# A list schedule with a margin on every transfer's landing time, and new tables of due times and earliest starts

## The chip, the cores and the metric

The kernel runs on one core of a Trainium2 chip. The metric is the device time of one execution in microseconds (us); of several executions the median is given. The engines are named as in the profile: PE multiplies matrices and PEld loads its weights, DVE and ACT do elementwise work, POOL and SP issue DMA transfers here and little else.

## The reference

One decoder block over 512 positions and 1024 channels, all in float32. `x` is (1, 512, 1024), `mem` (1, 256, 1024), and the inner width of the feed-forward part is 2816.

```
h = RMSNorm(x);  proj = h @ w_in          # 1024 x 9216: B, C, v | u, ug | q | three gates
y_a = (B * conv3(C * v)) @ w_a_out
y_b = swish(LayerNorm(conv31(u * sigmoid(ug)) + bias)) @ w_b_out
k, v = RMSNorm(mem) @ w_kv;  y_c = attention(q, k, v; 4 heads) @ w_att_out
m = sum_i sigmoid(gate_i + b_gate) * y_i
x = x + m @ w_o
f = RMSNorm(x) @ w_up;  gt, up = split(conv3(f))
out = RMSNorm(x + (silu(gt) * up) @ w_down)
```

All convolutions are depthwise and causal along the positions.

## The kernel before, in words

**Products.** A float32 product is made of three products of a faster format. A weight tile of 128x1024 is cast to its high part on ACT (`wh`, the tile `whi`, line 583), the low part is the difference on DVE (`wl`, the tile `wlo`, line 587), and the activations are split in the same way (`fh` and `fl`, lines 672 and 676; for the conformer branch by halves, lines 1459 and 1463). PE then adds up high times high, high times low and low times high (`multiply`, the matmuls at line 760).

**Quads.** The large projections go by quads: two column blocks by two row blocks of a weight are multiplied with seven products in place of eight, in the manner of Strassen. A quad `q` has the units (q,1), (q,2), (q,5), (q,6), (q,7), (q,4), (q,3), each of 24 matmuls of 256 columns, and the units of two neighbouring quads are interleaved. A unit's weight tile is a block as it stands in memory or the sum of two or more blocks. The four loads of a quad are `u`, `v`, `s` and `r`. Some sums are made by an accumulating DMA that POOL issues (`more`, line 708), which needs the earlier split of the same tile done. The results leave the PSUM banks by the reads `r1` to `r7` (`quad_reads`, lines 788 to 803 among them). The quads' names: `glu` and `cv` and `bb` for the short convolution's and the conformer's inputs, `q`, `gate`, `mq` for `w_b_out`, `up` and `down`; `wo` and `merge` are the plain products with `w_o` and `w_att_out`.

**Buffers.** Weights land in a ring of six slots (`wf`), in places also in the rings `sb` and `lf`; loads are issued by SP (`fetch_job`, line 613), the accumulating transfers by POOL. The split parts `whi` and `wlo` have four buffers each. A load goes out when its slot has been read for the last time, which is mostly the end of a `wl`.

**What sets the order.** PE's order is written out by hand (`seq`). Everything else is a job with an engine, a cost, the jobs that it comes after, and the slots that it takes. `latest_starts` works back from PE's order to a due time for each job and adds a shift from the table `LATER`, by the kind of job ("DVE wl up 3"). `run` then goes forward in a model of the time: of all jobs that are ready it takes the one that could start first, and of equals the one due first. The table `AHEAD` holds a kind of job back until so many us before its due time. For a transfer the model knows a cost and a latency (`LOAD, MORE = 1.42, 2.55` and `LOAD_LATENCY, MORE_LATENCY = 3.1, 3.4`), and lets SP and POOL share the bandwidth:

```
            ends[key] = free[e] + latency
            for k in dict.fromkeys(users.get(key, ())):
                waits[k] -= 1
                ready_at[k] = max(ready_at.get(k, 0.0), ends[key])
```

What comes out of `run` is only an order: the jobs' functions are called in it, and `issue_in_program_order` makes each engine issue its instructions as they were written. On the chip an engine waits only for the data and buffers that its next instruction needs, so a model time that is off shows as an instruction that stands too early in its engine's queue and holds up those behind it.

Of the kernel before, what the change touches and what calls it, by code (L numbers as in the profile page):

```python
# [67 lines left out]
TABLE_LOAD, TABLE_WAIT = 1.28, 3.0  # L68
SEEN = {"PE": 0.2, "ACT": 0.14, "DVE": 0.12}
# [11 lines left out]
    "ACT kh": 35, "ACT mgh a": -12.9, "ACT mgh c": -228, "ACT mgh d": -361.4, "ACT mgh e": -100,  # L81
    "ACT mgh g": 251.8, "ACT mh": -59.6, "ACT msq": 103.3, "ACT oh": -327, "ACT pth": 35,
# [6 lines left out]
    "ACT rt": -218.2, "ACT sg": -115, "ACT sigmoid": 1235, "ACT silu": -4.5, "ACT sq": -69,  # L89
    "ACT sr": -334, "ACT swish": 252, "ACT tap 1": -214.4, "ACT tap 2": -191, "ACT tap 3": -547.5,  # L90
# [8 lines left out]
    "ACT wn wo 0": -774.4, "ACT x root": 121, "ACT xroot": -5.5, "ACT xsq": -18, "ACT xsquare": 15,  # L99
# [8 lines left out]
    "DVE low": 39.7, "DVE m scale": -418, "DVE mgl a": 159, "DVE mgl b": 325.5, "DVE mgl d": 11,  # L108
    "DVE mgl e": 647.4, "DVE mgl g": -351, "DVE ml": 15, "DVE ms c": -142, "DVE ms d": -3.5,
    "DVE ms e": 328, "DVE msum": -143, "DVE mu fold": -89, "DVE mu low": -614, "DVE mu sum": -395,  # L110
    "DVE ol": -34, "DVE pn": -193, "DVE ptl": -147, "DVE ql": -1183.6, "DVE r2 bb": -176.3,
# [5 lines left out]
    "DVE rd f": -4, "DVE rd g": 51.4, "DVE sc": -297.1, "DVE sum": -988.2, "DVE tap 1": -30,  # L117
    "DVE tap 2": 25.4, "DVE tap 3": 51.2, "DVE top": -7.9, "DVE tot1": -8, "DVE tot2": -44,
    "DVE um": -1259, "DVE var fold": 4.7, "DVE var sum": -23.3, "DVE vl": 737, "DVE weigh": 547,
# [18 lines left out]
    "POOL s7 up": -142, "POOL wadd e": -277, "POOL wadd x": 2.1, "POOL wadd y": -65,  # L138
# [6 lines left out]
}  # L145

AHEAD = {
    "ACT fh h b00": 80, "ACT fh h b11": 150, "ACT fh h t4": 40, "ACT fh h t6": 40,
    "ACT fh h2 t4": 2, "ACT fh h2 t5": 5, "ACT fh h2 t6": 40, "ACT fh y b00": 10, "ACT fh y b10": 2,
    "ACT fh y t6": 80, "ACT m root": 40, "ACT mgh a": 2, "ACT mgh b": 40, "ACT mgh c": 2,  # L150
    "ACT mgh e": 5, "ACT pth": 40, "ACT qh": 20, "ACT r1 bb": 150, "ACT r1 q": 10, "ACT r1 up": 5,
    "ACT r4 gate": 5, "ACT r4 q": 2, "ACT r5 cv": 2, "ACT r5 gate": 40, "ACT r5 glu": 80,
    "ACT r5 q": 150, "ACT r5 up": 20, "ACT r6 bb": 5, "ACT r6 cv": 150, "ACT r6 gate": 20,
    "ACT r6 mq": 150, "ACT r6 q": 40, "ACT r6 up": 20, "ACT rb": 5, "ACT rh": 5, "ACT rm": 150,
# [53 lines left out]
class Jobs:  # L208
# [2201 lines left out]
```

## Time and profile before

Three runs took 941.35, 933.9 and 929.17 us; the median is 933.9. The profile belongs to another execution, the fastest that is known:

| | |
|---|---|
| median of three runs | 933.9 us |
| the profiled execution's own time | 926.63 us |
| its span | 924.8 us |
| mean granted clock of PE | 0.998 |
| PE busy | 911.2 us (99%), 6821 instructions |
| DVE busy | 849.1 us (92%), 973 instructions |
| ACT busy | 681.4 us (74%), 933 instructions |
| POOL busy | 137.2 us (15%), 165 instructions |
| DMA | 196.91 MB, 213 GB/s over the span |

The 1.8 us between 926.63 and 924.8 lie around the span. PE is busy nearly throughout, so what a change of the order can move is the idle time of PE, and that is read from the rows that give, for a PE instruction, how long it waited and for whom.

### The profile page before, as it was taken

How to read it: one execution, taken by the hardware profiler on the slowest of the kernel's cores; microseconds unless marked ns; L12 is line 12 of the kernel's file. 1: busy time of each engine (PE TensorE's matmuls, PEld its weight loads, DVE VectorE, ACT ScalarE, POOL GpSimd, SP SyncE). 2: the span in 40 equal slices, each digit the busy share in tenths (PEclk: the TensorE clock that was granted, in tenths of full speed). 3: DMA queues.
4: the chain of work that ended last, by engine and by line, in shares of the span. 5: the costliest groups of instructions: out<-in, count | busy, mean ns of one | idle time of the engine just before them, and what ended most of it. 6: DMA issues, size and time to landing. Idle time of an engine off the chain costs nothing.

```text
span 924.8 us, 17087 instructions
## 1 busy us (share of the span) xinstructions
PE 911.2 (99%) x6821; PEld 860.7 (93%) x6821; DVE 849.1 (92%) x973; ACT 681.4 (74%) x933; POOL 137.2 (15%) x165
## 2 busy tenths in 40 slices
PE   9999999999999999999999999999999999999996
PEld 8999999999989999999899997898999999988885
DVE  7898999999989999999876999987998889999977
ACT  7577988887988888569647983766766766765555
POOL 0011121100010121111100211121121111002400
PEclk9999999999999999999999999999999999999999
DMA  9999789764579798998957999899999786689962
GB/s 361 372 261 195 168 179 196 179 152 91 144 178 249 145 194 197 220 222 209 216 128 204 213 286 313 217 236 294 272 253 235 166 170 147 179 287 322 253 123 91
DMA packets 55951, 196.91 MB, mean 213 GB/s; under 512 B 6336, under 2 KB 6464, under 8 KB 55872
## 3 DMA queue, kind: packets, MB, share of 16 engines
q0 software_dynamic: 22608, 81.54, 49.6%
q1 hardware_dynamic: 32544, 113.23, 33.8%
q8 instruction: 53, 0.87, 0.4%
q10 hardware_dynamic: 720, 1.06, 0.3%
q14 instruction: 26, 0.21, 0.1%
HBM read 191.60 MB, written 4.19 MB: 212 GB/s over the span
## 4 chain that ended last, share of the span: by engine, by line
PE 84%; DVE 6%; DMA 5%; issue 2%; ACT 1%; SPq 0%; ACTq 0%; DVEq 0%; POOLq 0%
PE bank L760 52%; PE bank L535 6%; PE bank L536 6%; PE bank L534 6%; PE bank L1558 3%; PE bank L1559 3%; PE bank L1560 3%; DMA wf<-in_w_in 3%; DVE wlo L587 2%; PE bank L1017 2%; DMA wf<-in_w_up 2%; DVE upc L1514 1%; PE bank L1792 1%; DVE gtc L1514 1%; ACT whi L583 1%
## 5 line engine op out<-in xcount | busy, mean ns | idle before, releaser
L583 ACT CAST whi<-wf 128x1024 fp32r<-128x1024 f32 x204 | 212.0, 1043 | 101.3 <-PE bank L760 36.9
L587 DVE TENSOR_TENSOR wlo<-wf,whi 128x1024 fp32r<-128x1024 f32 x198 | 238.3, 1211 | 26.9 <-ACT whi L583 26.6
L1326 ACT ACTIVATE tp<-u,pk 128x510 f32<-128x510 f32 (+22 forms) x184 | 118.8, 705 | 2.8 <-DVE acc L1333 2.4
L1333 DVE TENSOR_TENSOR acc<-acc,tp 128x1022 f32<-128x1022 f32 (+22 forms) x92 | 109.1, 1188 | 4.1 <-ACT tp L1326 2.4
L708 POOL DMA_DIRECT2D wf<-in_w_in x50 | 44.4, 895 | 242.7 <-DVE wlo L587 163.0
L760 PE MATMUL bank<-ft6h,whi 128*128 128x256 f32 (+1 forms) x250 | 68.8, 276 | 1.1 <-ACT gt L788 1.1
L760 PE MATMUL bank<-ft4h,whi 128*128 128x256 f32 (+1 forms) x249 | 68.7, 276 | 0.9 <-DVE uu L540 0.9
L760 PE MATMUL bank<-ft5l,whi 128*128 128x256 f32 x248 | 68.7, 277 | 0.6 <-DVE ft5l L676 0.6
L760 PE MATMUL bank<-ft7h,whi 128*128 128x256 f32 x248 | 68.6, 277 | 0.7 <-ACT g L803 0.7
L760 PE MATMUL bank<-ft6h,wlo 128*128 128x256 f32 x248 | 68.7, 277 | 0.2 <-DVE wlo L587 0.2
L760 PE MATMUL bank<-fb10h,whi 128*128 128x256 f32 x248 | 68.7, 277 | 0.0
L760 PE MATMUL bank<-ft6l,whi 128*128 128x256 f32 x248 | 68.7, 277 | 0.0
L760 PE MATMUL bank<-fb00h,whi 128*128 128x256 f32 (+1 forms) x250 | 68.7, 276 | 0.0
L760 PE MATMUL bank<-fb11h,whi 128*128 128x256 f32 x248 | 68.7, 277 | 0.0
L760 PE MATMUL bank<-fb00l,whi 128*128 128x256 f32 x248 | 68.6, 277 | 0.0
L760 PE MATMUL bank<-ft5h,whi 128*128 128x256 f32 (+1 forms) x251 | 68.6, 275 | 0.0
L760 PE MATMUL bank<-ft4l,whi 128*128 128x256 f32 x248 | 68.6, 277 | 0.0
L760 PE MATMUL bank<-ft7l,whi 128*128 128x256 f32 x248 | 68.5, 276 | 0.0
L760 PE MATMUL bank<-ft7h,wlo 128*128 128x256 f32 x248 | 68.5, 276 | 0.0
L760 PE MATMUL bank<-ft4h,wlo 128*128 128x256 f32 x248 | 68.5, 276 | 0.0
L760 PE MATMUL bank<-fb11l,whi 128*128 128x256 f32 x248 | 68.5, 276 | 0.0
L760 PE MATMUL bank<-fb11h,wlo 128*128 128x256 f32 x248 | 68.5, 276 | 0.0
(400 smaller groups left out, 3157.7 us busy)
## 6 DMA issues: line engine op xcount, KB each, us to landing
wf<-in_w_in SPq DMA_DIRECT2D x53, 512.0 KB, 5.8
wf<-in_w_in POOLq DMA_DIRECT2D x50, 512.0 KB, 6.4
wf<-in_w_up SPq DMA_DIRECT2D x30, 512.0 KB, 7.7
wf<-in_w_up POOLq DMA_DIRECT2D x27, 512.0 KB, 7.3
wf<-in_w_down SPq DMA_DIRECT2D x15, 512.0 KB, 6.1
wf<-in_w_att_out SPq DMA_DIRECT2D x8, 512.0 KB, 4.2
wf<-in_w_a_out SPq DMA_DIRECT2D x8, 512.0 KB, 4.5
wf<-in_w_b_out SPq DMA_DIRECT2D x8, 512.0 KB, 6.0
```

The costliest lines, as they stand in the source:

```text
L534: nc.tensor.matmul(ps, s_hi, w_hi, start=start, stop=False, skip_group_check=again)
L535: nc.tensor.matmul(ps, s_hi, w_lo, start=False, stop=False, skip_group_check=again)
L536: nc.tensor.matmul(ps, s_lo, w_hi, start=False, stop=stop, skip_group_check=again)
L583: nc.scalar.copy(parts[0], src())
L587: nc.vector.tensor_tensor(lo, src(), hi.bitcast(F32), op=ALU.subtract)
L708: nc.gpsimd.dma_start(out=tiles[key], in_=block(w, col[c], k), accum_op=ALU.add)
L760: nc.tensor.matmul(ps[:, c, part], w[:, k, at], a[k][:, part], start=first and n == 0 and part.start == 0, stop=k == 3 and n == 2, skip_gr ...
L1326: nc.scalar.activation(two(("tp", p, s))[:, j, s:], two(("u", p))[:, j, : SEQ - s], AF.Copy, scale=weight(j),)
L1333: nc.vector.tensor_tensor(a, a, two(("tp", p, s))[:, :, s:], op=ALU.add)
L1558: nc.tensor.matmul(ps, w_hi[:, i, at], hi, start=first, stop=False)
L1559: nc.tensor.matmul(ps, w_hi[:, i, at], lo, start=False, stop=False)
L1560: nc.tensor.matmul(ps, w_lo[:, i, at], hi, start=False, stop=last)
```

## The change

A transfer lands later in the model by a margin, in both places where `run` sets its end: 1.2 us for a load of SP and 2.0 us for an accumulating transfer of POOL. The second of these places is where a transfer that is under way is slowed by one of the other queue. Both tables `LATER` and `AHEAD` have other numbers throughout; one line of each is kept here.

```diff
@@ -66,6 +66,7 @@
 TABLE_LOAD, TABLE_WAIT = 1.28, 3.0
+MARGIN = {"SP": 1.2, "POOL": 2.0}
 SEEN = {"PE": 0.2, "ACT": 0.14, "DVE": 0.12}
@@ -74,116 +75,118 @@
 LATER = {
-    "ACT kh": 35, "ACT mgh a": -12.9, "ACT mgh c": -228, "ACT mgh d": -361.4, "ACT mgh e": -100,
...
 AHEAD = {
...
+    "DVE fl h t6": 20, "DVE fl h t7": 10, "DVE fl h2 t5": 80, "DVE fl h2 t6": 5,
...
@@ -385,7 +388,7 @@
                     free[slowed] = self.moved(slowed, start)
-                    ends[other] = free[slowed] + self.jobs[other][4]
+                    ends[other] = free[slowed] + self.jobs[other][4] + MARGIN[slowed]
@@ -396,7 +399,7 @@
-            ends[key] = free[e] + latency
+            ends[key] = free[e] + latency + MARGIN.get(e, 0.0)
```

The program that comes out computes the same. PE's order is word for word the same, with 6693 rows. Of DVE's 899 jobs nearly all stand at another place or beside other neighbours. ACT loads its function tables 10 times and not 11. All lines behind the new one are numbered one or three higher.

**SP, at the loads of `w_b_out` and `w_o`** (the conformer branch's last product and the mixer's, from about half of the span on). The load for the unit (mq 1,1) is `wf_5876` before and `wf_5958` now; the quad's fourth load, r of (mq 1), is `wf_6235` before and `wf_6350` now. Before:

```order
L613 DMA wf_5780<-in_w_b_out 128x1024
L613 DMA wf_5844<-in_w_b_out 128x1024
L613 DMA wf_5876<-in_w_b_out 128x1024
L613 DMA wf_5888<-in_w_b_out 128x1024
L613 DMA wf_5922<-in_w_b_out 128x1024
L613 DMA wf_5958<-in_w_b_out 128x1024
L613 DMA wo_6183<-in_w_o 128x1024
L613 DMA wo_6192<-in_w_o 128x1024
L613 DMA wf_6226<-in_w_b_out 128x1024
L613 DMA wf_6235<-in_w_b_out 128x1024
```

After:

```order
L616 DMA wf_5780<-in_w_b_out 128x1024
L616 DMA wf_5845<-in_w_b_out 128x1024
L616 DMA wf_5881<-in_w_b_out 128x1024
L616 DMA wf_5891<-in_w_b_out 128x1024
L616 DMA wf_5926<-in_w_b_out 128x1024
L616 DMA wf_5958<-in_w_b_out 128x1024
L616 DMA wo_6181<-in_w_o 128x1024
L616 DMA wf_6190<-in_w_o 128x1024
L616 DMA wf_6224<-in_w_b_out 128x1024
L616 DMA wo_6232<-in_w_o 128x1024
L616 DMA wf_6312<-in_w_o 128x1024
L616 DMA wf_6350<-in_w_b_out 128x1024
```

The block that the unit (mq 1,1) multiplies was third and is sixth now, and the last load of `w_b_out` goes out behind four loads of `w_o` where there were two.

**ACT, at the same place** (the swish of the conformer branch, line 1424 before, and the casts behind it: `fb00h` is the activations' high part that (mq 1,1) needs, in two halves, and `whi` the weights'). Before:

```order
L1424 ACT_TABLE_LOAD
L1424 ACTIVATE acc_1093<-acc_1093,pk 128x512 x2
L1424 ACTIVATE acc_2140<-acc_2140,pk 128x512 x2
L1459 CAST ft5h_6030<-y_6002 128x512
L1459 CAST fb00h_6033<-acc_1093 128x512
L583 CAST whi_6038<-wf_5876 128x1024
L1459 CAST ft5h_6030<-y_6002 128x512
L1459 CAST fb00h_6033<-acc_2140 128x512
```

After:

```order
L1427 ACTIVATE acc_1093<-acc_1093,pk 128x512 x2
L1427 ACTIVATE acc_2144<-acc_2144,pk 128x512 x2
L586 CAST whi_6027<-wf_5958 128x1024
L1462 CAST fb00h_6032<-acc_1093 128x512
L1462 CAST fb00h_6032<-acc_2144 128x512
L1462 CAST ft5h_6039<-y_6035 128x512
L586 CAST whi_6066<-wf_5780 128x1024
```

The cast of the unit's weights now stands ahead of both halves of `fb00h`. On DVE the difference `wlo_6028` likewise stands ahead of `fb00l`, whose second half comes after `ft5l` and one more `wlo`.

**DVE, between the last quad of bb and the first of gate** (`B` from the bank is the read r7 of (bb,1); the `wlo` behind it belong to the units named in the text above, and `acc` with `tp` are taps of the conformer's convolution of 31 steps). Before:

```order
L540 SCALAR_TENSOR_TENSOR B_4509<-bank_4518,B_4509 128x2x256
L587 TENSOR_TENSOR wlo_4779<-wf_4091,whi_4778 128x1024
L1527 TENSOR_TENSOR C_4335<-C_4335,V_4263 128x1024
L1438 TENSOR_TENSOR yal_4817<-ya_3986,yah_4682 128x1024
L587 TENSOR_TENSOR wlo_4815<-wf_4442,whi_4814 128x1024
L1514 SCALAR_TENSOR_TENSOR ya_4819<-C_4335,pk,ya_4819 128x511
L1514 SCALAR_TENSOR_TENSOR ya_4819<-C_4335,pk,ya_4819 128x510
L587 TENSOR_TENSOR wlo_4849<-wf_4676,whi_4848 128x1024
```

After:

```order
L543 SCALAR_TENSOR_TENSOR B_4505<-bank_4510,B_4505 128x2x256
L590 TENSOR_TENSOR wlo_4747<-wf_4502,whi_4746 128x1024
L590 TENSOR_TENSOR wlo_4780<-wf_4057,whi_4779 128x1024
L1336 TENSOR_TENSOR acc_3850<-acc_3850,tp_4644 128x2x502
L590 TENSOR_TENSOR wlo_4813<-wf_4404,whi_4812 128x1024
L1336 TENSOR_TENSOR acc_3850<-acc_3850,tp_4740 128x2x501
L1537 TENSOR_TENSOR ya_4712<-ya_4712,B_4505 128x1024
L1321 SCALAR_TENSOR_TENSOR acc_3850<-u_1367,pk,acc_3850 128x500 x2
L1441 TENSOR_TENSOR yal_4887<-ya_4712,yah_4882 128x1024
L590 TENSOR_TENSOR wlo_4885<-wf_4541,whi_4884 128x1024
L590 TENSOR_TENSOR wlo_4890<-wf_4677,whi_4889 128x1024
```

`wlo_4849` before and `wlo_4890` now are the same unit, (gate (0,1),5): six instructions lie between it and r7 before, ten now, since the taps of the long convolution and three more `wlo` (units 2 and 7 of (gate (0,0)) among them) have come in between, and the `ya` steps and `C` have gone ahead of them.

More of the change, by code (lines that the diff above doesn't have):

```diff
@@ L76 @@
 LATER = {
[4 rows of a table removed]
-    "ACT kh": 35, "ACT mgh a": -12.9, "ACT mgh c": -228, "ACT mgh d": -361.4, "ACT mgh e": -100,
-    "ACT mgh g": 251.8, "ACT mh": -59.6, "ACT msq": 103.3, "ACT oh": -327, "ACT pth": 35,
[6 rows of a table removed]
-    "ACT rt": -218.2, "ACT sg": -115, "ACT sigmoid": 1235, "ACT silu": -4.5, "ACT sq": -69,
-    "ACT sr": -334, "ACT swish": 252, "ACT tap 1": -214.4, "ACT tap 2": -191, "ACT tap 3": -547.5,
[8 rows of a table removed]
-    "ACT wn wo 0": -774.4, "ACT x root": 121, "ACT xroot": -5.5, "ACT xsq": -18, "ACT xsquare": 15,
[8 rows of a table removed]
-    "DVE low": 39.7, "DVE m scale": -418, "DVE mgl a": 159, "DVE mgl b": 325.5, "DVE mgl d": 11,
@@ L138 @@
-    "POOL s7 up": -142, "POOL wadd e": -277, "POOL wadd x": 2.1, "POOL wadd y": -65,
[6 rows of a table removed]
+    "ACT c3": -1125, "ACT cf": 92, "ACT csq": -32.4, "ACT exp": -2553, "ACT fh h b00": 28,
[4 rows of a table added]
+    "ACT kh": -434, "ACT m root": -1788.7, "ACT mgh a": -521, "ACT mgh b": -746.8,
+    "ACT mgh c": 514.5, "ACT mgh d": -211, "ACT mgh e": 76, "ACT mgh g": -122, "ACT mh": -14.5,
+    "ACT msq": 8.3, "ACT mu high": -232, "ACT oh": -288.9, "ACT pth": 12, "ACT qh": -103.2,
[6 rows of a table added]
+    "ACT rm": 63.4, "ACT rt": -144, "ACT sg": -0.1, "ACT sigmoid": 157, "ACT silu": -42.6,
@@ new lines @@
+    "ACT sq": -63, "ACT sr": -487, "ACT tap 0": -32.2, "ACT tap 1": -558.2, "ACT tap 2": -296,
[8 rows of a table added]
+    "ACT wn wo 0": -272, "ACT x root": -323, "ACT xroot": -16, "ACT xsq": 1.4, "ACT xsquare": -187,
+    "ACT zh a": -10.6, "ACT zh b": 2.4, "ACT zh c": -6, "ACT zh d": 3, "ACT zh e": -80.2,
+    "ACT zh f": 203, "DVE CV": -7, "DVE c3": -391, "DVE centre": 299.7, "DVE cf": 226.9,
[6 rows of a table added]
+    "DVE hd": -972, "DVE kl": -93, "DVE kt": 11, "DVE lns": -431, "DVE low": 1.3,
+    "DVE m scale": -188.4, "DVE mgl a": -432, "DVE mgl b": 87, "DVE mgl c": -35, "DVE mgl d": 106,
@@ new lines @@
+    "DVE mgl e": -218, "DVE mgl g": -61, "DVE ml": 72.6, "DVE ms c": 56, "DVE ms d": 20,
+    "DVE ms e": 4, "DVE ms f": -343, "DVE msum": -84, "DVE mu fold": -5, "DVE mu low": 149,
+    "DVE mu sum": -10, "DVE ol": 18, "DVE pn": 12.7, "DVE ptl": -1112.3, "DVE ql": -414,
[5 rows of a table added]
+    "DVE rd g": -8.1, "DVE rl": 134.4, "DVE s6 glu": -220, "DVE sc": 110, "DVE sum": -57,
+    "DVE tap 0": 78.5, "DVE tap 1": 153.3, "DVE tap 2": -797, "DVE tap 3": 1168, "DVE top": -1053,
+    "DVE tot1": 13, "DVE tot2": 24.1, "DVE um": -162.8, "DVE v scale": -399.9, "DVE var fold": 6,
@@ L145 @@
+    "DVE var sum": -212.6, "DVE vl": 3848, "DVE weigh": 275.6, "DVE wl K 0": 0.3,
[7 rows of a table added]
+    "DVE x1 g": 47, "DVE xn": -396.1, "DVE xnorm": -164, "DVE xsum": -728.4, "DVE y t4": -2.6,
[3 rows of a table added]
+    "POOL ea": -4.1, "POOL s3 bb": -15, "POOL s3 gate": -17.2, "POOL s3 glu": -564,
[5 rows of a table added]
+    "POOL wadd x": 13.5, "POOL wadd y": -190, "POOL wl merge 0": 15, "POOL wl merge 2": 7.8,
[6 rows of a table added]
 }
 AHEAD = {
-    "ACT fh h b00": 80, "ACT fh h b11": 150, "ACT fh h t4": 40, "ACT fh h t6": 40,
-    "ACT fh h2 t4": 2, "ACT fh h2 t5": 5, "ACT fh h2 t6": 40, "ACT fh y b00": 10, "ACT fh y b10": 2,
@@ L150 @@
[L150 to L154, printed above, removed]
-    "ACT rt": 10, "ACT sq": 150, "ACT tap 1": 10, "ACT tap 2": 20, "ACT tap 3": 150,
[4 rows of a table removed]
@@ L160 @@
-    "ACT wn merge 0": 5, "ACT xroot": 40, "ACT xsquare": 150, "ACT zh c": 150, "ACT zh g": 5,
-    "DVE CV": 80, "DVE c3": 80, "DVE centre": 150, "DVE ends": 150, "DVE fl h b00": 150,
[5 rows of a table removed]
-    "DVE ol": 150, "DVE pn": 20, "DVE ptl": 40, "DVE ql": 5, "DVE r2 glu": 20, "DVE r2 q": 5,
-    "DVE r2 up": 40, "DVE r3 gate": 150, "DVE r3 glu": 80, "DVE r3 q": 10, "DVE r7 bb": 20,
-    "DVE r7 gate": 20, "DVE r7 glu": 2, "DVE r7 mq": 10, "DVE r7 up": 40, "DVE rd a": 40,
-    "DVE rd c": 2, "DVE rd d": 150, "DVE rd f": 40, "DVE sum": 150, "DVE top": 5, "DVE tot1": 20,
[5 rows of a table removed]
@@ L176 @@
-    "DVE xnorm": 150, "DVE xsum": 5, "DVE y t4": 10, "DVE y t5": 150, "DVE y t6": 10,
[5 rows of a table removed]
-    "POOL wadd x": 150, "POOL wadd y": 80, "POOL wl merge 0": 10, "POOL wl merge 2": 20,
[4 rows of a table removed]
+    "ACT c3": 80, "ACT cf": 150, "ACT csq": 10, "ACT fh h b10": 2, "ACT fh h b11": 5,
+    "ACT fh y b10": 80, "ACT fh y b11": 10, "ACT fh y t4": 150, "ACT fh y t6": 5, "ACT fh y t7": 80,
+    "ACT high": 80, "ACT kh": 10, "ACT m root": 20, "ACT mgh a": 80, "ACT mgh b": 10,
+    "ACT mgh e": 80, "ACT mgh g": 80, "ACT mh": 150, "ACT mu high": 2, "ACT qh": 2, "ACT r1 cv": 80,
[3 rows of a table added]
@@ new lines @@
+    "ACT swish": 10, "ACT tap 1": 20, "ACT tap 2": 150, "ACT tap 3": 2, "ACT tp 2": 150,
[4 rows of a table added]
+    "ACT x root": 2, "ACT xroot": 5, "ACT xsquare": 20, "ACT zh d": 40, "ACT zh g": 5,
[4 rows of a table added]
+    "DVE h2 t6": 5, "DVE h2 t7": 2, "DVE kl": 80, "DVE kt": 150, "DVE lns": 2, "DVE m scale": 5,
+    "DVE mgl a": 5, "DVE mgl c": 10, "DVE mgl d": 150, "DVE mgl e": 80, "DVE ml": 150,
+    "DVE ms c": 80, "DVE ms e": 80, "DVE mu sum": 80, "DVE ol": 150, "DVE pn": 80, "DVE ptl": 40,
[4 rows of a table added]
+    "DVE sum": 150, "DVE tap 2": 20, "DVE tot2": 40, "DVE v scale": 40, "DVE wl K 0": 80,
[8 rows of a table added]
@@ L187 @@
+    "POOL s7 bb": 80, "POOL s7 gate": 40, "POOL s7 glu": 10, "POOL s7 up": 80, "POOL wadd x": 150,
[4 rows of a table added]
 }
```

6 lines of the change are left out of this document (removed), and 154 rows, old and new, of tables (AHEAD, LATER).

## The prediction

> **What bounds the kernel now.** First the page's engine line and its clock line, then the waits of PE, then two windows:
>
> ```profile
> span 924.8 us, 17087 instructions
> PE 911.2 (99%) x6821; PEld 860.7 (93%) x6821; DVE 849.1 (92%) x973; ACT 681.4 (74%) x933; POOL 137.2 (15%) x165
> PEclk9999999999999999999999999999999999999999
> ```
> ```profile
> PE bank L1958 <- POOL ident masks.py:199: 1.4, 1, 1.4
> PE bank L760 <- ACT gt L788: 1.1, 1, 1.1
> PE bank L760 <- DVE uu L540: 0.9, 1, 0.9
> PE bank L535 <- DVE wlo L587: 0.8, 1, 0.8
> PE bank L760 <- ACT g L803: 0.7, 1, 0.7
> PE bank L760 <- DVE ft5l L676: 0.6, 1, 0.6
> PE bank L760 <- DVE wlo L587: 0.2, 1, 0.2
> ```
> ```profile
> 500.00:525.00 25.00, 25.00 (x193) 23.84 (x192) 22.17 (x27) 23.89 (x34) 6.12 (x7) 1.00 0.87 202
> 916.00:924.90 8.90, 0.97 (x9) 0.77 (x7) 2.73 (x7) 3.41 (x9) 0.00 (x0) 0.81 0.47 179
> ```
>
> PE is the bound. Its waits come to 5.7 us in all, in seven places. The first, 1.4, is the start, and the last window shows that about 7.9 us at the end are without PE: the closing norm and the output, whose order stays. So the other six waits, 1.1 + 0.9 + 0.8 + 0.7 + 0.6 + 0.2 = 4.3 us, are all that an order of the other engines can take away. With PE's own order unchanged this gives a floor of 926.6 - 4.3 = 922.3 us for an execution like the profiled one. It can lose far more: DVE is busy for 92%, ACT fills 23.89 of 25 us around 500, and any operand that comes late stops PE, since its order is fixed. The sum below is therefore a list of the places where the new order makes an operand late. I found them by putting the two orders beside each other: for each piece, DVE's and ACT's new rows with the durations that the old trace has for them, from an instruction whose place in time is the same in both.
>
> **The margin itself** costs no time on the chip: it is a number in the model that only chooses an order. It removes and adds no transfer and no elementwise work. One of eleven table loads goes, from ACT's stretch before swish. There the term below is decided by a load and not by ACT, so I count it as nothing; if ACT decided, the swish would only come earlier, which is inside the lower bound of that term.
>
> **The start, +0.7.** PE takes up (glu 0),2 at 47.37 without a wait. Its `wlo` was ready long before:
>
> ```profile
> 40.67 1.21 DVE L587 TENSOR_TENSOR wlo<-('glu', 0)_48_332,whi 128x1024 fp32r<-128x1024 f32 x1
> 47.37 0.28 PE L760 MATMUL bank<-fb10h,whi 128*128 128x256 f32 x1
> ```
>
> It now stands behind `fb00l`, `fb10l` and an `h`, 6.2 us later in DVE's work: 40.67 + 1.21 + 6.2 = 48.1, against 47.37. Bounds 0 (the order before it may run earlier) and +1.2, one more instruction of this kind.
>
> **The stretch from bb to gate, +0.9.** In the old trace:
>
> ```profile
> 390.05 1.23 DVE L587 TENSOR_TENSOR wlo<-wf,whi 128x1024 fp32r<-128x1024 f32 x1
> 391.19 0.69 DVE L540 SCALAR_TENSOR_TENSOR B<-bank,B 128x512 f32<-128x512 f32 x1
> 392.35 0.28 PE L760 MATMUL bank<-ft4h,whi 128*128 128x256 f32 x1
> 398.17 1.23 DVE L587 TENSOR_TENSOR wlo<-wf,whi 128x1024 fp32r<-128x1024 f32 x1 [0.31 <-ACT whi L583]
> 403.23 0.28 PE L760 MATMUL bank<-ft5h,whi 128*128 128x256 f32 x1
> 406.81 0.39 PE L760 MATMUL bank<-ft7h,whi 128*128 128x256 f32 x1 [0.69 <-ACT g L803]
> 423.25 0.28 PE L760 MATMUL bank<-ft5h,whi 128*128 128x256 f32 x1
> ```
>
> The `wlo` at 398.17 is that of (gate (0,1),5), used at 403.23, 3.8 us after its end. In the new order the work between r7 of (bb,1) (391.19) and it grows from 6 to 10 instructions. Walked with 1.14 us from a 1024-wide instruction's start to the next (390.05 to 391.19) and half of it for the 512-wide ones, r7 itself ends about 0.4 late and the `wlo` at 404.2, 0.6 after the 403.6 at which PE would then want it. The next quad's unit 5 repeats this at 423.25, +0.6. Against it r6 comes in time at 406.81, and 0.7 are won: 0.4 + 0.6 + 0.6 - 0.7 = +0.9. Bounds 0 and +2.
>
> **The loads of w_b_out, +2.5, the largest term.**
>
> ```profile
> 502.13 1.23 DVE L587 TENSOR_TENSOR wlo<-wf,whi 128x1024 fp32r<-128x1024 f32 x1 [4.01 <-ACT whi L583]
> 507.00 2.94 ACT L1424 ACTIVATE acc<-acc,pk 128x512 f32<-128x512 f32 x4
> 513.26 0.68 DVE L1463 TENSOR_TENSOR fb00l<-acc,fb00h 128x512 fp32r<-128x512 f32 x1
> 515.33 0.28 PE L760 MATMUL bank<-fb00h,whi 128*128 128x256 f32 x1
> ```
> ```profile
> wf<-in_w_b_out SPq DMA_DIRECT2D x3, 512.0 KB, 8.7
> wo<-in_w_o SPq DMA_DIRECT2D x2, 512.0 KB, 7.2
> wo<-in_w_o POOLq DMA_DIRECT2D x2, 512.0 KB, 13.1
> ```
>
> The second fence is the DMA view of 500 to 525, in us from issue to landing. The load of (mq 1,1) moves from third to sixth. Its slot is then freed by the `wlo` that ends at 502.13 + 1.23 = 503.4, and with 8.7 us it lands at 512.1. Its cast stands ahead of both halves of `fb00h` on ACT, so these wait too: cast to 513.1, `wlo` to 514.3, then `fb00l`, `ft5l`, another `wlo` and the second `fb00l`, 0.6 + 0.6 + 1.14 + 0.7 after one another with the casts that feed them, to 517.7. PE wants it at 515.33: +2.5 with the wake-up. If the load lands before the swish is done, at 507.00 + 2.94, DVE's chain alone leaves +0.4; with the 13.1 us of the slowest row it is 13.1 - 8.7 = 4.4 more, +6.9. I take 8.7, the row of this very queue, tensor and time. Behind this wait on ACT stand the other casts of mq, which the stall of PE lets catch up.
>
> The Trainium skill (DMA: Bandwidth & Descriptors, section "Anatomy of one DMA — SWDGE (gpsimd) path") fits a transfer by 2.0 us and its bytes at 436 GB/s, by which 512 KB take an estimated 3.2 us. By that the load is there at 506.6 and this term falls to +0.4, and no margin would be wanted at all; the rows of 7.2 to 13.1 disagree, and I go by them.
>
> **The last load of w_b_out, +0.5.** Behind four `w_o` loads it waits for a slot that is freed late, at about 532.5 and not 524.5, lands at 541 with the same 8.7, and is needed at 545 and, after the stall, at 547.7. That is 7 us for a cast, a `wlo` and whatever stands before them: 0 to +4, taken as +0.5. The accumulating `w_o` transfers that move back on POOL keep over 20 us and cost nothing; if that cover went, 13.1 us each.
>
> **The first up quads, 0.0.**
>
> ```profile
> 639.93 0.36 PE L760 MATMUL bank<-ft4h,whi 128*128 128x256 f32 x1 [0.90 <-DVE uu L540]
> 642.75 0.28 PE L760 MATMUL bank<-fb11h,whi 128*128 128x256 f32 x1
> 646.74 0.39 PE L760 MATMUL bank<-ft6h,whi 128*128 128x256 f32 x1 [1.11 <-ACT gt L788]
> ```
>
> `uu` comes as late as before. The `wlo` of the next unit moves behind the five conv steps and ends near 644.1, a new stall of about 1.6 at 642.75; in turn the waits at 646.74, 1.1 and 0.2 behind it, are covered by it. Net between -0.1 and +1.5; I take 0, since the stall moves and the chain of work before (up 2,6) is the same length.
>
> **A load of up near the end, 0.0.**
>
> ```profile
> 792.62 0.33 SPq L613 DMA_DIRECT2D wf<-in_w_up  x1
> 798.30 0.33 SPq L613 DMA_DIRECT2D wf<-in_w_down  x1
> 803.07 1.06 ACT L583 CAST whi<-wf 128x1024 fp32r<-128x1024 f32 x1
> wf<-in_w_up SPq DMA_DIRECT2D x1, 512.0 KB, 4.0
> ```
>
> The load of 792.62 now goes out behind the one of 798.30 and lands at 798.4 + 4.0 = 802.4, just ahead of its cast at 803.07. With the 7.7 us that is the median of all up loads it would be +3.
>
> ```profile
> wf<-in_w_up SPq DMA_DIRECT2D x30, 512.0 KB, 7.7
> ```
>
> **The sum** is 0.7 + 0.9 + 2.5 + 0.5 + 0 + 0 = +4.6: 931.2 for an execution like the profiled one, 926.6. The timed median, 933.9, lies 7.3 above that, and the three timed runs spread over 12 us, which the trace of one execution doesn't explain; the likeliest cause is landing times that vary, to which fixed orders with little slack are exposed. Loads that the model believes later are ordered with more slack, so I let half of this excess stand, 3.7: 931.2 + 3.7 = 934.9, say 935.
>
> **Rivals.**
>
> *The margin pays.* The old waits vanish and none of my new ones comes, because the rows ahead of my places run earlier than I think: 922.3, and 924 to 930 with the spread of the timed runs. For it speaks that every wait of PE that names a read or a `wlo` is one that a better order could lift; against it, that five of my six walks find an operand later than before.
>
> *The late loads decide, slower.* One mechanism: (mq 1,1) and the casts queued behind it on ACT wait for a load issued at 503.4, and the last w_b_out load does the same 30 us on. From a landing of about 6.5 us on, the load and not DVE sets the end; at the 13.1 of the POOL row the terms are 6.9 and 4 and more, together with the start and gate 12.5 and, since landings are then late elsewhere too, the whole excess: 926.6 + 12.5 + 7.3 = 946.4, and 949.4 where the up load of 798 lands late as well (+3). For it speaks the DMA share of 0.87 there; against it, that SP's own rows are 7.2 and 8.7.
>
> *The change does nothing that counts.* A load goes out when its slot is free, whatever its due time:
>
> ```profile
> SPq L613 <- DVE wlo L587: 597.2, 117, 17.5
> ```
>
> SP waits 597 of 924.8 us for a `wlo`, so margins reorder mainly what has slack anyway: 933.9.
>
> *A long stall slows the clock.* At the start matmuls of 256 columns begin 0.21 apart and then 0.12:
>
> ```profile
> 6.61 0.37 PE L1017 MATMUL bank<-ml,whi 128*128 128x256 f32 x1
> 6.82 0.28 PE L1017 MATMUL bank<-mh,wlo 128*128 128x256 f32 x1
> 6.94 0.28 PE L1017 MATMUL bank<-mh,whi 128*128 128x256 f32 x1
> ```
>
> If a stall of PE in the middle brought the slow rate back for some 15 matmuls, each such stall would cost about 15 x 0.1 = 1.5 us more, and two of them would give 938. The Trainium skill (TensorE: Matmul & The Clock Gate, section "Part 1: The HAM clock gate") lets an idle window of about 3.4 us halve the clock; by that my 2.5 us would just escape it and the rival's 6.9 not. The clock line, nine throughout, shows no such case in this trace.
>
> **How the numbers follow.** The forecast of traded stalls, 935, gets 0.52; the margin that pays 0.25; late loads 0.10; nothing that counts 0.10; the clock 0.03. About 2% is what a measurement of this kernel can tell from no change, that is below 915.2 or above 952.6. Nothing reaches the first, as the floor is 922.3: 0.02 for a mistake in that. The second is reached where every bound goes the wrong way (+1.2 + 2 + 6.9 + 4 + 1.5 + 3 = 18.6, with 7.3 again 952.5) and one place that I have not walked adds to it, of some 900 moved jobs: most of the late loads' 0.10, and a little of the forecast's, 0.10 together. The rest, 0.88, is within 2%. The range goes from the floor, 922.5, to 952, and leaves out that last case and little else.
>
> **What would show it.** Right: PE's waits name `fb00l` or `wlo` near 515 with 2 to 3 us, a `wlo` near 643 and 404, the start at 48, and no read of `gt` near 647; PE's busy time stays at 911 and its idle time rises by 4 to 5. Wrong: PE's waits sum to under 4 us (the margin pays), the wait near 515 is over 5 (late loads), PEclk falls below nine in a slice, or the span differs in its last 8 us.

## The result and the profile after

The changed kernel takes 925.7 us (median of 22 executions, 924.19 to 931.45), the kernel before in the same session 931.4 (22 executions, 926.44 to 941.35). The ratio is 0.9957, with a 95% interval of 0.9937 to 0.9978: faster by 0.4%, well inside the 2% that counted as no change. It is a ratio of means and leaves out the one execution of 941.35, which lies more than 1.5% above the fastest; the medians are 0.6% apart. The forecast was 935, 1.1 us slower than the 933.9 of three runs, so its direction was wrong, while its range and its main chance (0.88 for "within 2%") held.

The profiled execution took 925.68 us, only 0.95 less than that of before. First the page's lines and PE's waits of the changed kernel, in the same columns as before:

```profile
span 923.9 us, 17125 instructions
PE 911.9 (99%) x6821; PEld 861.8 (93%) x6821; DVE 847.4 (92%) x973; ACT 681.9 (74%) x932; POOL 137.5 (15%) x165
PEclk9999999999999999999999999999999999999998
```
```profile
PE bank L1961 <- POOL ident masks.py:199: 1.4, 1, 1.4
PE bank L763 <- DVE y L543: 0.8, 1, 0.8
PE bank L763 <- DVE wlo L590: 0.7, 1, 0.7
PE bank L538 <- DVE wlo L590: 0.7, 1, 0.7
PE bank L763 <- DVE fb10l L1466: 0.3, 1, 0.3
```

Without the start PE waits 2.5 us in four places, where it waited 4.3 in six. The waits for `gt`, `uu`, `g` and `ft5l` are gone, and new are one for `y` at 546 and one for `fb10l` at 527, both in the conformer's last product, and one for a `wlo` at 629.6. Waits account for 1.8 us; the medians are 5.8 apart. The rest does not stand in these two profiles, and the experiments look for it.

Over the whole study the kernel before was run 174 times: median 930.8, quartiles 928.1 and 933.6, highest 942.7. The changed kernel was run 34 times: 26 of them at 924.1 to 926.9 and 8 at 929.7 to 931.5, with nothing between. Its gain is thus two things: a lower floor (about 924 against 926) and a far narrower spread with one upper group. The median of before lay between 928.8 and 933.4 in the six sessions, so a kernel is compared by its ratio to the before of its own session.

### The profile page after: what moved, and what is told of

The parts are those of the page before. It is cut to its first block, busy times and chain, and to the rows that moved or that the text cites. A ratio compares the mean times of both kernels' runs of the same rounds, so it can differ in the third digit from the quotient of the medians.

```text
span 923.9 us, 17125 instructions
## 1 busy us (share of the span) xinstructions
PE 911.9 (99%) x6821; PEld 861.8 (93%) x6821; DVE 847.4 (92%) x973; ACT 681.9 (74%) x932; POOL 137.5 (15%) x165
## 4 chain that ended last, share of the span: by engine, by line
PE 95%; DVE 2%; DMA 2%; ACT 1%; SPq 0%; issue 0%; ACTq 0%; DVEq 0%
PE bank L763 61%; PE bank L538 6%; PE bank L539 6%; PE bank L537 6%; PE bank L1563 3%; PE bank L1562 3%; PE bank L1561 3%; PE bank L1020 2%; DMA wf<-in_w_up 1%; DVE wlo L590 1%; PE bank L1795 1%; DMA wf<-in_w_v 1%; PE ss L893 0%; PE bank L1850 0%; PE bank L1257 0%; ACT whi L586 0%
## 5 line engine op out<-in xcount | busy, mean ns | idle before, releaser
L1329 ACT ACTIVATE tp<-u,pk 128x511 f32<-128x511 f32 (+22 forms) x184 | 119.5, 709 | 5.0 <-DVE acc L1336 4.9
L763 PE MATMUL bank<-fb10l,whi 128*128 128x256 f32 x248 | 68.6, 276 | 0.3 <-DVE fb10l L1466 0.3
```

What stands on the lines that cost most here:

```text
L763: nc.tensor.matmul(ps[:, c, part], w[:, k, at], a[k][:, part], start=first and n == 0 and part.start == 0, stop=k == 3 and n == 2, skip_gr ...
L1329: nc.scalar.activation(two(("tp", p, s))[:, j, s:], two(("u", p))[:, j, : SEQ - s], AF.Copy, scale=weight(j),)
```

## The experiments

**Both kernels again.** No edit; a second profile of each, and more times.

> The kernel before once more, for a second profile and more times. Theory A (the gain lies in executions whose landings are late): the times spread again over 926 to 935 with a median near 931, and this profile, if it falls on an execution above 930, shows waits of PE that the first one (4.3 us without the start) does not have, each ending in a tile that a transfer filled; their sum explains the excess within 1 us. Rival B (the spread has nothing to do with waits, for example a rate of the matmuls): a profile above 930 has the same waits and a PE busy time above 913.

> The changed kernel once more. Its times fell into two groups, 924 to 927 and 930 to 931.5. Theory A: median 925.5 +- 1, two groups again; if the profile falls into the upper group, one place with about 5 us of waiting on a transfer stands in it that the first profile lacks. Rival B: no such place, and the 5 us are spread.

Before: median 928.9 (near 931 was expected), 926.6 to 930.7, profiled at 928.66. Changed: 924.9, eleven executions at 924.1 to 926.2 and one at 930.88, profiled at 924.27. The second profile of before has the waits of the first and more, in the stretch from bb to gate:

```profile
PE bank L760 <- ACT g L803: 1.4, 1, 1.4
PE bank L760 <- ACT B L803: 0.7, 1, 0.7
```

The first was 0.7 in the first profile and the second not listed. On ACT the read `g` (line 803) stands behind a chain that begins with a cast waiting for a load. In columns start, duration, instruction, and in brackets the idle time and what ended it:

```profile
399.46 1.05 ACT L583 CAST whi<-wf 128x1024 fp32r<-128x1024 f32 x1 [2.00 <-DMA wf<-in_w_in]
406.64 1.06 ACT L1434 CAST yah<-ya 128x1024 fp32r<-128x1024 f32 x1 [2.83 <-DVE ya L1534]
408.55 0.58 ACT L803 COPY g<-bank 128x512 f32<-128x512 f32 x1
```

In the first profile the first two of these waited 1.56 and 2.10, and the read started at 406.19. A load that comes later makes the read later, and PE waits for it. Neither profile fell on an execution above 930, so rival B stayed open here; a profile of a spliced kernel, below, bears it out.

**Margin and tables apart.**

```diff
 # b_margin: the kernel before, its own LATER and AHEAD
+MARGIN = {"SP": 1.2, "POOL": 2.0}
-            ends[key] = free[e] + latency
+            ends[key] = free[e] + latency + MARGIN.get(e, 0.0)
 # (and the other place in run)
 # a_nomargin: the changed kernel
-MARGIN = {"SP": 1.2, "POOL": 2.0}
+MARGIN = {"SP": 0.0, "POOL": 0.0}
```

> The margin alone: before's tables, 1.2 and 2.0 us in run. Theory A (the margin makes the gain): median 924 to 928, spread as narrow as the changed kernel's (under 8 us). Rival C (the tables make the gain; they only fit the model that they were drawn up with): the old tables under another model give an order with new waits of PE, 935 or more, at any rate not below 930.

> The tables alone: the changed kernel with both margins at zero. Theory A: back near 931, with a spread of 10 us or more. Rival C (an order is good where tables and model belong together): above 930 too, but by waits that its profile shows (PE waits over 8 us without the start). Rival D (the new tables alone make the gain): 924 to 928.

The margin alone: 962.9 us, ratio 1.034 (1.030 to 1.039), slower. The tables alone: 939.2, ratio 1.010 (1.006 to 1.014), slower, by less than 2%. So neither half makes the gain; rival C holds (in the profile of the tables alone PE waits 9.2 us for other engines without the start, where over 8 was expected). The waits of the margin alone show what an order looks like whose tables were drawn up for another model:

```profile
PE bank L535 <- ACT whi L584: 9.1, 1, 9.1
PE bank L535 <- DVE x L1822: 3.5, 1, 3.5
```

The profile of the tables alone gave the clue to the spread. It took 946.97 us, the six other executions 937.3 to 941.2. From 700 to 740 us its PE is busy throughout at full clock, yet 342 matmuls fall into it where the changed kernel has 356 (the columns are the window, its length, PE busy and count, PEld, DVE, ACT, POOL, clock, DMA share, GB/s; first the tables alone, then the changed kernel):

```profile
700.00:740.00 40.00, 40.00 (x342) 40.00 (x341) 34.83 (x41) 25.87 (x32) 6.96 (x8) 1.00 0.90 214
```
```profile
700.00:740.00 40.00, 40.00 (x356) 40.00 (x355) 34.49 (x41) 27.83 (x35) 7.78 (x9) 1.00 1.00 241
```

By the start times in the traces a matmul of 256 columns begins every 0.113 us at the one pace and every 0.118 at the other, 4% apart, and it is not the granted clock, which is 1.00 in both. Whole stretches run at the one pace or the other.

**A split matmul as a reset.**

```diff
         halved = long_rows(seq[here - 1]) and isinstance(seq[here + 1][0], tuple)
+        halved = halved or q[0] == "up" and f == 4
```

The kernel already issues the first matmul of a unit as two of 128 columns where it follows products with 512 columns; here that is done eleven times more.

> The changed kernel, with the first matmul of unit 4 of each of the eleven up quads issued as two of 128 columns (11 more instructions, same work). The times of both kernels fall into two groups about 5.5 us apart. Theory P (pace): after a stall PE can go on with 0.118 us between matmuls in place of 0.113 until something resets it, 4.5 ns x 1366 matmuls of the last undisturbed up stretch = 6.1 us; a split matmul resets it, so the upper group vanishes, all times lie at 924 to 927.5. Rival L (a late landing makes the upper group): the two groups stay, a quarter of the times at 929.5 to 931.5. If the split toggles the pace and does not set it, the profile alternates from quad to quad and the time is about 3 us up in all executions.

> The same eleven splits in the kernel before. Theory P: its upper group (932 to 936, about a third of the times) vanishes, the lower stays at 926 to 931, median 928. Rival L: nothing changes, median 930 to 931.5.

In the changed kernel the upper group is gone: 12 executions at 925.3 to 927.4, median 926.2. The eleven splits cost about 1 us together (the median of the lower group was 925.2), so the median is no better, but P's expectation was met and L's was not. With 8 of 34 in the upper group, twelve executions without it would come by luck in some 4% of cases; later runs add to them. In the kernel before the splits leave 928.3 to 934.2, median 930.7, ratio 0.9997 (0.997 to 1.0024): the expectation failed there, something else spreads it too.

**The two orders spliced.** The jobs are called in a list that is written out: the one order up to a certain product of PE, the other's order for all jobs that are left. 

```diff
-            best = None
-            for e in free: ...
+            key = order.pop()      # before's jobs up to (up 0,1), then the rest as the change has them
```

> The order of before up to the first product of up, and from there the changed kernel's order for all jobs that are left. By the waits of the profiles the new order saves 2.4 us in up and down (before: 0.8 + 0.9 + 1.1 + 0.2 and 0.4 of slow starts behind them, after: 0.9) and nothing sure before it. Theory W (the gain is the waits in up): median 925 to 927. Rival M (the gain lies in the stretch before up, where before loses 0.7 to 3 us between 386 and 407): 928 to 931.

> The changed kernel's order up to the first product of up, and from there that of before. Theory W: the waits of up are back, median 928 to 931. Rival M: 924.5 to 926.5. If both halves gain, both of these kernels lie between 925.5 and 929.

| first | from | then | median us | lowest | highest | ratio to before, 95% |
|---|---|---|---|---|---|---|
| before | up, 595 us | change | 931.7 | 923.6 | 938.3 | 0.9985 (0.9946 to 1.0024) |
| change | up, 595 us | before | 927.0 | 926.6 | 932.7 | 0.9960 (0.9929 to 0.9991) |
| before | gate (0,1), 403 us | change | 935.9 | 930.0 | 939.3 | 1.0048 (1.0020 to 1.0077) |
| change | cv 1, 289 us | before | 929.0 | 928.2 | 938.3 | 1.0008 (0.9979 to 1.0037) |
| change | gate (1,1), 475 us | before | 926.4 | 925.8 | 932.2 | 0.9956 (0.9929 to 0.9982) |

The first two rows part the gain. The old order in up and down raises the floor by 1.6 us (926.8 for nine of twelve executions, against 925.2 for the changed kernel's lower group), near the 2.4 that theory W put on the waits there: theory W, for the floor. The old order ahead of up leaves a floor of 923.6 but spreads to 936.6 and once to 938.3: theory M, for the spread and the median. Each theory had half in kind; neither had the medians, since 931.7 lies above both ranges and 927.0 between them.

The profile of the first row fell on an execution of 934.02 us and shows the slow pace begin. PE's matmuls there, line 865:

```profile
632.21 0.28 PE L865 MATMUL bank<-ft4h,whi 128*128 128x256 f32 x1
632.33 0.28 PE L865 MATMUL bank<-ft4l,whi 128*128 128x256 f32 x1
632.44 0.34 PE L865 MATMUL bank<-ft4h,wlo 128*128 128x256 f32 x1
632.62 0.28 PE L865 MATMUL bank<-ft4h,whi 128*128 128x256 f32 x1
...
632.97 0.28 PE L865 MATMUL bank<-ft4h,whi 128*128 128x256 f32 x1
633.09 0.28 PE L865 MATMUL bank<-ft4l,whi 128*128 128x256 f32 x1
633.21 0.28 PE L865 MATMUL bank<-ft4h,wlo 128*128 128x256 f32 x1
```
```profile
660.00:700.00 40.00, 40.00 (x342) 40.00 (x341) 37.32 (x44) 26.33 (x34) 7.88 (x9) 1.00 1.01 241
740.00:780.00 40.00, 40.00 (x342) 40.00 (x341) 33.79 (x40) 26.27 (x33) 5.19 (x6) 1.00 0.66 139
```

One matmul takes 0.34 us and not 0.28, since its `wlo` comes just as it is needed, and the next starts 0.07 late. From there they start 0.118 apart and not 0.113, 342 in 40 us where the other has 355, until up ends at about 810. That is 3.7% of 178 us, some 6.5 us for a hiccup of 0.07. The DMA share is 1.01 in the one window and 0.66 in the other, so the slow pace here does not hang on how busy the transfers are. PE's line on this page:

```profile
PE 919.9 (99%) x6821; PEld 870.3 (93%) x6821; DVE 849.3 (91%) x973; ACT 683.1 (73%) x933; POOL 137.4 (15%) x165
```

PE is busy for 8.7 us more than in the first profile of before, while its waits without the start are 3.1 us and not 4.3. So rival B of "Both kernels again" had this right: above 930, the excess is here in the rate of the matmuls. The profiles of the third and fourth rows, at 935.94 and 937.57 us, have 918.7 and 920.9 us of busy time.

A late operand does not always start the slow pace, and it can end it. In the first profile of before PE waits 0.90 and 1.11 us at 640 and 647 and goes on at the fast one (355 matmuls from 660 to 700). In that of the changed kernel the slow pace begins behind the wait of 0.75 at 629.58 and ends at a matmul that is held up by 0.05:

```profile
646.64 0.33 PE L763 MATMUL bank<-ft6h,wlo 128*128 128x256 f32 x1
631.00:645.00 14.00, 14.00 (x122) 14.00 (x121) 10.82 (x14) 8.27 (x11) 2.65 (x3) 1.00 1.05 329
650.00:664.00 14.00, 14.00 (x126) 14.00 (x125) 13.86 (x17) 11.01 (x16) 2.29 (x4) 1.00 1.04 251
```

In the last version below, with three splits and a move, PE is held up for 0.15 us at 644.95, goes on at the slow pace, and has the fast one again from the split matmul (128x128, x2) on:

```profile
675.91 0.34 PE L866 MATMUL bank<-ft4h,whi 128*128 128x128 f32 x2
650.00:674.00 24.00, 24.00 (x206) 24.00 (x205) 22.97 (x29) 17.18 (x22) 3.89 (x5) 1.00 1.04 256
678.00:702.00 24.00, 24.00 (x214) 24.00 (x213) 21.07 (x25) 16.78 (x22) 6.12 (x7) 1.00 0.97 246
```

The kernel with 30 splits (below) shows the same at 415.0. The upper group of the changed kernel lies 5.2 us above its lower one (930.4 against 925.2), which is near the 6.5. No profile fell on an execution of that group, so that the slow pace makes it is inferred from its size and from the splits that take it away.

**Where before up.** Three of the rows of the table above, and splits in the first matmul of unit 4 of every quad (the condition is `f == 4` alone, 30 splits).

> The order of before up to unit (gate (0,1),5) at 403 us, the changed kernel's for all that is left. If the spread arises before 403 (theory E, early): median 928 to 931, times over 8 us apart, as in the kernel that changes over at up (931.7). If it arises between 403 and up (theory F): median 925 to 926.5, two groups as in the changed kernel.

> The changed kernel's order up to (cv 1,5) at 289 us, that of before for the rest. Spread from 0 to 289: as the kernel that changes over at up, median 927, lower group within 1.5 us. Spread from 289 on: median 929 to 932, times over 8 us apart.

> The changed kernel's order up to (gate (1,1),5) at 475 us, that of before for the rest. Spread from 289 to 475: median 927, lower group within 1.5 us and a few times at 932.5. Spread from 475 to up: median 929 to 932.

> The kernel before with the first matmul of unit 4 of every quad split, 30 in all, so that a slow pace ends after 19 us at most anywhere. 30 splits at 0.1 us cost about 3. If the spread before up is the pace (theory P there too): all times within 4 us, at 928.5 to 932.5. If it is waits that vary from one execution to the next: times still 7 us or more apart, median 932 to 934.

With the changed order up to 475 us the old one costs nothing but the floor of up. With it up to 289 only, the lower group rises from 926.4 to 928.4 and five of twelve executions lie at 931 to 938. So what the old order does between 289 and 475 is worth 2 us of floor (0.4 of it a wait at the joint, at 292, that neither kernel has) and part of the spread. The third row is not clean: behind its joint, at 420.7, PE waits 2.3 us, which it does in neither kernel, and its median of 935.9 lies above both expectations. But its profile shows the earliest place. On ACT a cast waits for an accumulating transfer of glu, and the read `ug` behind it keeps PE:

```profile
66.01 1.05 ACT L688 CAST whi<-('glu', 0)_58_378 128x1024 fp32r<-128x1024 f32 x1 [1.66 <-DMA ('glu', 0)_58_378<-in_w_in]
66.96 1.05 ACT L777 CAST fb11h<-hb 128x1024 fp32r<-128x1024 f32 x1
70.96 0.58 ACT L908 COPY ug<-bank 128x512 f32<-128x512 f32 x1
71.59 0.39 PE L865 MATMUL bank<-ft7h,whi 128*128 128x256 f32 x1 [1.24 <-ACT ug L908]
80.00:120.00 40.00, 40.00 (x342) 40.00 (x342) 35.00 (x37) 33.65 (x46) 6.93 (x8) 1.00 0.73 148
```

In the first profile of before this cast ran 2.6 us earlier and the read was in time, with 356 matmuls in the same window. In the changed kernel two of the five instructions that stood between them come after the read, which ends at 68.24, 1.6 us before PE's unit begins:

```profile
67.66 0.58 ACT L806 COPY ug<-bank 128x512 f32<-128x512 f32 x1
68.14 1.06 ACT L586 CAST whi<-('glu', 0)_90_538 128x1024 fp32r<-128x1024 f32 x1
```

The 30 splits took the kernel before to 932.3, 929.95 to 934.2. They raise the lowest time of the session by 3.9 us, where 3 was expected, and leave 4.2 between lowest and highest (12 executions), where before has 14.8 in the same session (35 executions). So much of the old order's spread is the pace, and up to 4 us are left for the waits. How much of it arises ahead of up is not settled: the eleven splits in up alone had left 5.9 (12 executions).

**Reads moved ahead of late work.** In the kernel before, with its order written out, single jobs are moved and nothing else.

```diff
 # ACT, b_r6: at two places
-L1434 CAST yah<-ya           # waits for DVE's ya, which waits for a load
 L583 CAST whi<-wf
 L803 COPY B<-bank (g<-bank)  # the read r6 that PE waits for
+L1434 CAST yah<-ya
 # b_fix: besides, fb11h, fb11l and the cast of (glu 0,4) behind the read ug, a yal behind the read r7 of (bb,1)
 # b_r6h: b_r6 and eleven splits in up; b_fixs: b_fix and six splits
```

> The kernel before with two casts moved on ACT: each of two yah casts (line 1434), which wait for DVE's ya behind a late load, goes from two places ahead of a PSUM read (r6 of (bb,1) and of (gate (0,0)), line 803) to right behind it. Nothing else moves. Theory G (before's broad spread comes from this read standing behind work that waits for a landing): PE's waits for B L803 and g L803 (0.7 in one profile of before, 2.1 in another) are gone, the lowest times stay at 925.5 to 926.5, the values between 927 and 931 move down to 926 to 928, and a group 5 to 6 us higher stays; median 927 to 929. Rival: the load's lateness only passes to the next wait of PE (a wlo of gate), the times stay as they were, 930 to 931.

> The same two moves and the eleven split matmuls in the up stretch. If G and P together are the whole account of before's spread, all times lie within 4 us, at 926.5 to 930.5, median 928 (the splits cost about 1). If either is missing a factor, values above 932 remain as in the kernel with the splits alone (928.3 to 934.2).

> The kernel before with five moves and nothing else: on ACT the two yah casts of the earlier experiment behind the reads r6 of (bb,1) and (gate (0,0)), the casts fb11h and that of (glu 0,4) behind the read r6 of (glu,0); on DVE fb11l after it, and the low part of ya behind the read r7 of (bb,1). The reads then stand directly ahead of what does not wait for a transfer. If the reads' places are the cause of the spread before up: lower group 926 to 928, an upper group near 932 from the waits in up, median 927 to 928.5. If not: median 929 to 931 and 8 us or more between the lowest and the highest, as before.

> The same five moves with six split matmuls: in unit 4 of glu 2, of gate (0,1) and (1,0), and of up 1, 3 and 5. If order and pace are the whole account: all times within 4 us, at 926.5 to 930.5, median 927.5. If something else spreads the old order: still times above 932.

| | median us | lowest | highest | ratio to before, 95% |
|---|---|---|---|---|
| b_r6 | 929.7 | 926.7 | 939.2 | 0.9968 (0.9937 to 0.9999) |
| b_r6h | 930.6 | 928.9 | 937.2 | 0.9983 (0.9956 to 1.0011) |
| b_fix | 930.7 | 926.8 | 938.8 | 1.0018 (0.9991 to 1.0045) |
| b_fixs | 929.4 | 927.4 | 933.8 | 1.0003 (0.9979 to 1.0028) |

The moves did not do what theory G said. In the profile of the five moves the wait for `g` of line 803 is gone, and in its place stands one for `g` from DVE, a read some 6 us on, at 412:

```profile
PE bank L862 <- DVE g L642: 0.7, 1, 0.7
```

In that of the two moves the waits for `B` and `g` of line 803 are gone too, and PE waits 0.7 for `B` from DVE. Here the lateness that one read no longer meets is met by another instruction. Splits narrow the spread again (6.4 between lowest and highest with them and 12.0 without, 8.2 and 12.5 in the other pair), moves by hand do not.

**Three splits in the changed kernel, and a move.** The splits stand behind its last long wait (`(q, f)` in unit 4 of up 1, 3 and 5), and with them goes a move on DVE of the read r7 of (mq,1) ahead of the `wlo` that the last load of `w_b_out` keeps waiting.

> The changed kernel with three split matmuls only, in unit 4 of up quads 1, 3 and 5, the first of them behind its last long wait. Theory P: no time above 928, median 924.5 to 925.5, mean 925 against 926.4 of the changed kernel; by the rival the upper group at 930 keeps a quarter of the times.

> The changed kernel with the three splits and one move on DVE: the read r7 of (mq,1) ahead of the wlo of (mq 1,4), which waits for the cast of the last load of w_b_out. The wait of PE of 0.8 to 0.9 us at 545 falls to 0.0 to 0.3; median 924 to 924.8, all below 927.5. If the wlo is as late as the read, the wait only changes its name.

With the splits: 925.25 (924.3 to 926.2, seven executions), ratio to before 0.9917 (0.9887 to 0.9947), no upper group, mean 925.4 against the changed kernel's 926.4. With the move too: 925.0 (923.6 to 925.5, six executions), ratio 0.9908 (0.9878 to 0.9939); the wait for `y` is no longer among PE's waits, but between these two the difference is too small to tell. Both are ahead of the kernel before. That they are ahead of the changed kernel is not shown: the intervals of the ratios overlap, and the changed kernel's own second session had a mean of 925.45.

## Why the prediction was wrong, by its own steps

From the 935 of the forecast to the measured 925.7 it is 9.3 us, and two steps make them up: the sum over places, which gave +4.6 where the two profiles differ by -0.95 (5.6 us), and the scatter that was let stand (3.7). Either of them alone, put right, would have turned the direction: 929.4 or 931.2 against 933.9.

**What bounds the kernel** was right: PE's busy time differs by 0.7 us between these two profiles, and no execution of any kernel here came under the floor of 922.3. What it left out is that PE's busy time itself can grow, by 8.7 us in the profile of the first spliced kernel.

**The start, +0.7, and the stretch from bb to gate, +0.9: nothing of either.** The rows of the changed kernel:

```profile
46.23 1.22 DVE L590 TENSOR_TENSOR wlo<-('glu', 0)_41_297,whi 128x1024 fp32r<-128x1024 f32 x1
47.87 0.28 PE L763 MATMUL bank<-fb10h,whi 128*128 128x256 f32 x1
391.04 0.68 DVE L543 SCALAR_TENSOR_TENSOR B<-bank,B 128x512 f32<-128x512 f32 x1
400.84 3.49 DVE L590 TENSOR_TENSOR wlo<-wf,whi 128x1024 fp32r<-128x1024 f32 x3
```

The `wlo` of the start ends at 47.45 and not 48.1, that of (gate (0,1),5), the second of the three at 400.84, at 403.2 and not 404.2; its unit starts at 403.74. The step that failed is the walk's anchor: it took DVE's old start times as the place from which to add up the new instructions, while the new order also moved work away ahead of it. A walk of some ten instructions is good to about 1 us, and both terms were smaller than that. The 0.7 credited there, the wait at 406.8, did go.

**The loads of w_b_out, +2.5: nothing.** This is the largest term that failed.

```profile
483.88 19.35 SPq L616 DMA_DIRECT2D wf<-in_w_b_out  x6
wf<-in_w_b_out SPq DMA_DIRECT2D x6, 512.0 KB, 5.2
509.31 1.05 ACT L586 CAST whi<-wf 128x1024 fp32r<-128x1024 f32 x1 [0.51 <-PE bank L1562]
514.52 0.68 DVE L1466 TENSOR_TENSOR fb00l<-acc,fb00h 128x512 fp32r<-128x512 f32 x1
515.65 0.28 PE L763 MATMUL bank<-fb00l,whi 128*128 128x256 f32 x1
```

The load goes out as the last of six that end at 503.2, as was walked. But the median landing is 5.2 us (view of 480 to 505) where 8.7 was taken, the cast runs at 509.3 and not 512.1, held up last by PE and not by the load, and the second half of `fb00l` is ready at 515.2, in time for the eighth matmul of the unit, the first that reads it. The row of the same queue and tensor had three transfers in it, in another mix of loads: too few for the largest term. The 5.2 lie between these 8.7 and the 3.2 that the prediction set aside; the latter come from a fit for transfers of POOL, as the section that it names says in its title, while this load is SP's. The term's own lower bound, +0.4, was the better figure.

**The last load of w_b_out, +0.5**, is the term that came out, with some luck, since 0.5 was picked from bounds of 0 to 4: PE waits 0.75 at 546.30.

```profile
543.24 2.01 ACT L586 CAST whi<-wf 128x1024 fp32r<-128x1024 f32 x2 [0.49 <-DMA wf<-in_w_b_out]
544.33 1.23 DVE L590 TENSOR_TENSOR wlo<-wf,whi 128x1024 fp32r<-128x1024 f32 x1 [0.33 <-ACT whi L586]
546.30 0.36 PE L763 MATMUL bank<-ft4h,whi 128*128 128x256 f32 x1 [0.75 <-DVE y L543]
```

The casts wait for the load, DVE's `wlo` for the cast, and PE for the read `y` behind it; the load's lateness arrived by way of a third instruction.

**The first up quads, 0.0**, came out below the lower bound of -0.1: the waits of 1.1, 0.9 and 0.2 were not traded but went, for one of 0.75 at 629.58; by the spliced orders up is worth 1.6 us. The `wlo` of 643 ended at 643.5 and not 644.1, again the anchor. **The load of up near the end, 0.0**, held: no wait of PE is listed behind 629.58.

**The scatter, +3.7, is the other step that failed.** The prediction halved the 7.3 us between the profile of before and its timed median, and called late landings the likely cause. Of these 7.3 us 3.1 were the chance of three executions: by 174 the median is 930.8. And most of the rest went, not half: the median lay 4.8 us above the lowest time before (930.8 and 926.0), and lies 1.5 above it now (925.6 and 924.1). The cause is in part another than landings: a late operand costs its wait and then, in some executions, the slow pace until something ends it. That the order decides how often fits the spliced orders; which of its instructions do so is open.

**The rival "the margin pays"**, at 924 to 930 with a chance of 0.25, had the time right, and the sign that the prediction gave for it came: PE's waits are 2.5 us, or 3.9 with the start, and so under 4. That it is the margin that pays is not shown: without its tables it costs 3.4%.

**The clock rival** had the place right, a stall of PE that is followed by slower matmuls, and the mechanism wrong: the granted clock is 1.00 in the slow windows, the loss is 3.7%, lasts for 178 us in one profile and follows there a hiccup of 0.07 us. The Trainium skill (TensorE: Matmul & The Clock Gate, section "Part 1: The HAM clock gate") ties slow matmuls to idle windows of 3.4 us and a halved clock; the runs show a loss that this rule does not cover.

**Open** remain which of the old order's waits between 289 and 475 us matter (of six jobs moved by hand three lie there, and the median did not fall), what in PE sets the pace and why a late operand starts it, ends it or leaves it, and whether another pair of margin and tables would do as well: one pair was compared, not a family.

## What to carry to other kernels

Where the timed median lies well above the profiled execution, the two are different executions, and the difference has to be looked for before a change is priced from the profile: look at the list of times for groups, and count matmuls per window in a profile of the upper one. A term that is smaller than the error of the walk that gave it, here about 1 us, should stand in the range and not in the sum. A schedule's margin and its fitted tables are one thing; changed apart they cost 1% and 3.4%, and together they gave 0.4%.

## What the runs showed of the hardware

Matmuls of 256 columns run at one of two paces at the same granted clock of 1.00, 355 or 342 in 40 us. A late operand of 0.07 us was enough to change from the fast to the slow one; it then held for 178 us. Another of 0.05 us brought the fast one back, and waits of 0.90 and 1.11 us changed nothing. A first matmul issued as two of 128 columns, at about 0.1 us each, brought the fast pace back in the two places where a trace shows one behind slow matmuls (675.9 and 415.0). With it in every up quad, and with three of them, no execution of the changed kernel (25 in all, the version with the move counted, in other sessions) fell into the upper group, where 8 of 34 did without.
